# A one-core mLSTM and attention trunk: zero products ahead of TensorE's queue, the first scale row on SP's queue, far loads held back

## The chip, the cores and the metric

The kernel runs on one core of a Trainium2 chip. The metric is the device time of one execution in microseconds (us). TensorE (PE) multiplies matrices, VectorE (DVE) and ScalarE (ACT) do the elementwise work, GpSimd (POOL) and SyncE (SP) here mostly issue DMAs. PEld is TensorE's loading of the fixed operand, which overlaps its products.

## The reference

A trunk of two layers works on x (512 rows of 1024 float32). Each layer has a mixer, a cross-attention into 256 memory rows and a gated feed-forward block, and every block stands between two RMS norms:

```python
for layer in range(DEPTH):                     # DEPTH = 2
    hn = rms_norm(x, g[0])
    y = mlstm_mixer(hn, ...) if layer % 2 == 0 else stick_breaking_mixer(hn, ...)
    x = x + rms_norm(y, g[1])
    y = memory_cross_attention(rms_norm(x, g[2]), mem_n, ...)
    x = x + rms_norm(y, g[3])
    y = swiglu_ffn(rms_norm(x, g[4]), ...)
    x = x + rms_norm(y, g[5])
def rms_norm(x, gain):
    return x * rsqrt(mean(x * x) + 1e-6) * gain
```

## The kernel before

Every float32 operand of a product is split into a rounded high part and the remaining low part, and one product is made of three (low by high, high by low, high by high). ACT makes the high part with a cast, DVE the low part with a subtraction (`split`, `halves`). Most of the large products use `seven`: a 2 by 2 block product in seven block products in place of eight. It loads three of four weight blocks with SP and lets POOL add the fourth onto a block that is already there, in place, by an accumulating DMA (`gather`). So a `gather` has to wait until every reader of the block is done. In `seven` one PSUM bank `w` collects several block products, and between two of them its partial sum is copied out to a half-size buffer (`aside`).

The program is written as a list of operations in program order. `Plan.lay_out` gives them their place: it keeps a planned clock for PE, DVE, ACT, POOL and SP, and at each step takes the operation that can start first, by rank (when PE will want its result). Buffers come from a few slots per kind: 44 `big` (128 rows of 1024 floats), 8 `half`, 2 `gain` (a row of scales spread over 128 partitions, for the norms), 64 `sm`, 8 `ps` (PSUM banks). The order that comes out is fixed: each engine runs its own list strictly in that order, and a slot that is not free makes the engine wait, and with it all that stands behind on that engine.

At the start x comes in four tiles of 128 rows on SP's queue, the first in two halves, and between them come the first weights (`w_tm` of `ml_w_in`). Tile by tile `arrive` normalises (`sumsq` on ACT, a chain of small DVE and ACT operations, then on DVE x times scale times gain), turns the tile over with TensorE (`transpose_half`, the products of line 519), and splits the result; then come the first products (line 505). The gain row of this first norm, `g0`, is loaded by POOL. The mixer's gates are worked out beside this on a few rows: ACT copies a bank of 36 rows, DVE runs scans over 4 rows, and TensorE turns the result over in ten and four small products (4x4).

Of the kernel before, what the change touches and what calls it, by code (L numbers as in the profile page):

```python
# [8 lines left out]
F32 = mybir.dt.float32  # L9
R = mybir.dt.float32r  # L10
# [6 lines left out]
P = 128  # L17
D = 1024
S = 512
# [26 lines left out]

BY_DMA = (1, 3, 4)
LATER = 1000
OS = 4000
QUARTERS = (1, 6)  # L50
PROJECT = (1, 0, 1, 1, 1, 2, 0, 0)
# [79 lines left out]
class Plan:  # L131
# [63 lines left out]
    def lay_out(self):  # L195
# [25 lines left out]
                        b.lacks += sum(d not in b.group for d in o.deps)  # L221

        def feasible(o, e, headrank):
            t = max(free[e], o.ready)
            need = {}
            for b in o.bufs:
                if b.slot is None and b.kind in SLOTS:
                    need[b.kind] = need.get(b.kind, 0) + 1
                    if b.lacks and o.rank > headrank:
                        return None  # L230
            for k, n in need.items():
                s = slots[k]
                ahead, spare = SCARCE.get(k, (0, 0))
                if o.base <= headrank + ahead:
                    spare = 0
                elif spare and o.base > headrank + 25000:
                    return None
                if len(s) < n + spare:
                    return None
                t = max(t, s[n + spare - 1][0] + 60)  # L240
            return t
# [3 lines left out]
        while left:  # L245
            while head < len(pe_order) and pe_order[head].start is not None:
                head += 1
            headrank = pe_order[head].rank if head < len(pe_order) else float("inf")
            for e in free:
                found = None  # L250
                n = 0
# [26 lines left out]
            e = min((x for x in free if best[x]), key=lambda x: best[x][0], default=None)  # L278
# [6 lines left out]
            t, o = best[e]  # L285
# [87 lines left out]
class Trunk:  # L373
# [383 lines left out]
            self.ts(b[:, i : i + 1], ss, m / D, m * EPS, ALU.mult, ALU.add)  # L757
        return b[:, 0:1], b[:, 1:2]

    def gain(self, row):  # L760
        g = self.plan.buf("gain", (P, D))
        self.dma("POOL", g, row.broadcast_to([P, D]))
        return g

    def prenorm(self, out, x, g, steps=False):
        ss = self.small(1)
        self.sumsq(x, ss)
        if steps:
            v, r = self.small(1), self.small(1)
            self.ts(v, ss, 1.0 / D, EPS, ALU.mult, ALU.add)  # L770
            self.rsqrt(r, v)
        else:
            r = self.rstd(ss, D)
        self.stt(out, x, r, g, ALU.mult, ALU.mult)
# [365 lines left out]
    def stick(self, h, w_qkv, w_out, filler, finish):  # L1140
# [92 lines left out]
        def open_pair(qk):  # L1233
            z, sp = {}, {}
            for e in range(2):
                s = {}
                for b, parts in (("c", ((e, 2, 0),)), ("b", ((e, 1, 0), (e, 3, 384))), ("a", ((e, 0, 0),))):
                    z[b, e], s[b] = scores(parts, qk), self.half(S)
                    sp[b, e] = tiles(S)
                    softplus(z[b, e], s[b], sp[b, e][:, 0 : z[b, e].free])  # L1240

                u = s["c"][:, 128:256]
                self.tt(u, u, s["b"][:, 384:512], ALU.add)
                self.split(sp["c", e][:, 256:384], u)
            return z, sp

        ot, os_, qk = [], [], [project(0), project(1)]
        for p in range(KD):
            z, sp = open_pair(qk[p])
            with self.sooner(OS):  # L1250
                for o in ot[len(os_):]:
                    os_.append(self.both((S,)))
                    self.split(os_[-1], o)
            with self.later(LATER):
                for _ in range(PROJECT[p]):
# [271 lines left out]
def trunk_kernel(tc, x, mem, mem_norm_gain, norm_gains, ml_w_in, ml_b_gate, ml_head_gain, ml_w_out,  # L1527
                 sb_w_qkv, sb_w_out, xa_w_q, xa_w_kv, xa_w_o, ffn_w_gate_up, ffn_w_down, out):
    k = Trunk()
    x, mem, out = x[0], mem[0], out[0]  # L1530
    depth = norm_gains.shape[0]
    mem_gain = mem_norm_gain.rearrange("(o d) -> o d", o=1)

    def g(layer, i):
        return k.gain(norm_gains[layer, i : i + 1])

    xin = [k.big(D) for _ in range(NT)]
    for c in (slice(0, 512), slice(512, D)):
        k.dma("SP", xin[0][:, c], x[0:P, c], 700)
    for t in range(1, NT):  # L1540
        k.dma("SP", xin[t], x[t * P : (t + 1) * P])
    g0 = g(0, 0)
    k.constants()
    h = k.blocks()

    def arrive(t):
        if t:
            k.prenorm(xin[t], xin[t], g0)
            k.transpose_into(h, t, xin[t])
            return  # L1550

        ss, halves = k.small(2), [slice(0, 512), slice(512, D)]
        for i, c in enumerate(halves):
            k.sumsq(xin[t][:, c], ss[:, i : i + 1])
        r = k.rstd(ss[:, 1:2], D, k.rest(ss[:, 0:1]))
        for i, c in enumerate(halves):
            k.stt(xin[t][:, c], xin[t][:, c], r, g0[:, c], ALU.mult, ALU.mult)
            k.transpose_half(h, t, xin[t][:, c], i)

    spill = None  # L1560
    for layer in range(depth):
        j = layer // 2
        nxt, kt = {}, []

        def filler(n):

            if n and "m" not in nxt:
                nxt["m"] = k.memory(mem, mem_gain)
            for hh in range(len(kt), min(XAH, len(kt) + n)):
                kt.append(k.memory_keys(nxt["m"], xa_w_kv[layer], hh))  # L1570

        def after_mixer(n, t, ps):
            if "f" not in nxt:
                if "m" not in nxt:
                    nxt["m"] = k.memory(mem, mem_gain)
                xs = []
                for tt in range(NT):
                    xt = k.big(D)
                    k.dma("POOL", xt, x[tt * P : (tt + 1) * P] if spill is None else spill[tt])
                    xs.append(xt)  # L1580
                nxt["xs"] = xs
                nxt["h"] = k.blocks()
                nxt["f"] = k.boundary(xs, g(layer, 1), g(layer, 2), nxt["h"])
            nxt["f"](n, t, ps)

        if layer % 2 == 0:
            k.mlstm(h, arrive, ml_w_in[j], ml_b_gate[j : j + 1], ml_head_gain[j : j + 1], ml_w_out[j], filler, after_mixer)
        else:
            k.stick(h, sb_w_qkv[j], sb_w_out[j], filler, after_mixer)
        xs, h = nxt["xs"], nxt["h"]  # L1590
        nxt2 = {}

        def after_cross(n, t, ps):
            if not nxt2:
                nxt2["h"] = k.blocks()
                nxt2["x"] = [k.plan.buf("dr", (P, D)) for t in range(NT)]
                nxt2["f"] = k.boundary(xs, g(layer, 3), g(layer, 4), nxt2["h"], spill=nxt2["x"])
            nxt2["f"](n, t, ps)

        k.cross(XORDER[layer], h, nxt["m"], kt, filler, xa_w_q[layer], xa_w_kv[layer], xa_w_o[layer], after_cross)  # L1600
        h = nxt2["h"]
        nxt3 = {}

        def after_ffn(ys):
            xs = [k.big(D) for _ in range(NT)]
            for x, kept in zip(xs, nxt2["x"]):
                k.dma("POOL", x, kept)
            if layer == depth - 1:
                return k.boundary(xs, g(layer, 5), None, None, ys=ys, out=out)
            nxt3["h"] = k.acts()  # L1610
            nxt3["x"] = [k.plan.buf("dr", (P, D)) for t in range(NT)]
            return k.boundary(xs, g(layer, 5), g(layer + 1, 0), nxt3["h"], ys=ys, spill=nxt3["x"])

        k.ffn(UNITS[layer], h, ffn_w_gate_up[layer], ffn_w_down[layer], after_ffn)
        if layer < depth - 1:
            h, spill = nxt3["h"], nxt3["x"]
    k.plan.lay_out()
    k.plan.emit(tc)
# [24 lines left out]
```

## Time and profile before

| | |
|---|---|
| three runs | 1495.31, 1495.33, 1497.83 us; median 1495.33 |
| the profiled execution | 1499.86 us, of which the span of its instructions is 1498.2 |
| busy in the span | PE 1470.4 us (98%), DVE 1214.7 (81%), ACT 863.6 (58%), POOL 142.6 (10%) |
| DMA | 190.46 MB, mean 127 GB/s |
| chain that ended last | PE 31% of the span, all other engines together under 1% |

Matmuls are pipelined, so "busy" on PE is not the same as running at its peak. Idle time of an engine that nobody waits for costs nothing. Where a row names a releaser (`<-`), it is the one whose signal came last.

### The profile page before, as it was taken

The page shows a single profiled execution, that of the slowest core. Times are in us where ns is not written, and L with a number is a line of the kernel's source. Part 1 is how long each engine was busy: PE and PEld are TensorE (multiplying, and loading weights), DVE is VectorE, ACT ScalarE, POOL GpSimd, SP SyncE. Part 2 cuts the span into 40 slices and gives each one's busy share as a digit, 9 for nine tenths or more (in the row PEclk, how much of TensorE's full clock was granted, in tenths as well). Part 3 has the DMA queues.
Part 4 walks back from the last instruction along what each step waited for, and adds up shares of the span by engine and source line. Part 5 has one row for each costly group of instructions (what it writes and reads, how often), then busy time and mean ns, then how long its engine had stood idle before and what let it go on. Part 6 is the DMA issues. An engine that isn't in the chain of part 4 may idle for free. (4 is left out here: it accounts for less than half of the span.)

```text
span 1498.2 us, 26046 instructions
## 1 busy us (share of the span) xinstructions
PE 1470.4 (98%) x10346; PEld 1372.4 (92%) x10346; DVE 1214.7 (81%) x1920; ACT 863.6 (58%) x1533; POOL 142.6 (10%) x179
## 2 busy tenths in 40 slices
PE   6999899999999999999999999999999999999998
PEld 5999889998999999998889889888988999999996
DVE  7978879797887876888858998879787969768985
ACT  6668746474754454635548897756456635444632
POOL 2100100100111110110100000000000111110110
PEclk9999999999999999999999999999999999999999
DMA  7545747342654665565511215336514573854651
GB/s 240 113 85 115 223 129 237 71 128 85 203 107 100 132 150 129 118 145 187 166 32 29 71 45 182 113 119 175 143 57 140 116 167 58 205 119 86 141 170 56
DMA packets 166810, 190.46 MB, mean 127 GB/s; under 512 B 6944, under 2 KB 140576, under 8 KB 166688
## 3 DMA queue, kind: packets, MB, share of 16 engines
q1 hardware_dynamic: 119632, 121.16, 25.4%
q0 software_dynamic: 47056, 67.64, 23.0%
q8 instruction: 81, 1.33, 0.4%
q14 instruction: 41, 0.34, 0.1%
HBM read 176.72 MB, written 10.49 MB: 125 GB/s over the span
## 5 line engine op out<-in xcount | busy, mean ns | idle before, releaser
L505 PE MATMUL ps<-big,big 128*128 128x256 f32 (+2 forms) x9712 | 1407.3, 305 | 7.0 <-ACT big L436 3.5
L505 PEld LDWEIGHTS ps<-big,big 128*128 128x128 f32 x9712 | 1294.1, 189 | 93.5 <-ACT big L436 3.9
L451 DVE TENSOR_TENSOR big<-big,big 128x1024 fp32r<-128x1024 f32 (+1 forms) x516 | 607.2, 1210 | 48.9 <-ACT big L436 30.0
L436 ACT CAST big<-big 128x1024 fp32r<-128x1024 f32 (+1 forms) x385 | 391.2, 1044 | 139.9 <-DMA big<-in_ffn_w_gate_up_dram 42.1
L429 ACT ACTIVATE half<-ps 128x512 f32<-128x512 f32 (+4 forms) x185 | 92.5, 527 | 108.0 <-PE ps L505 99.7
L436 ACT COPY half<-ps 128x512 f32<-128x512 f32 (+2 forms) x105 | 61.4, 585 | 137.6 <-PE ps L505 124.9
L451 DVE TENSOR_TENSOR big<-ps,big 128x512 fp32r<-128x512 f32 (+3 forms) x188 | 109.6, 603 | 32.5 <-ACT big L436 20.3
L436 ACT CAST big<-ps 128x512 fp32r<-128x512 f32 (+2 forms) x164 | 80.2, 516 | 91.8 <-PE ps L505 55.2
L451 DVE TENSOR_TENSOR big<-half,big 128x512 fp32r<-128x512 f32 (+3 forms) x150 | 82.7, 575 | 9.3 <-ACT big L429 7.6
L429 ACT ACTIVATE half<-big 128x512 bf16<-128x512 f32 (+1 forms) x63 | 41.9, 665 | 73.1 <-DVE big L451 47.0
L418 POOL DMA_DIRECT2D big<-in_ffn_w_gate_up_dram x40 | 50.8, 1271 | 330.6 <-DVE big L451 171.1
L463 DVE SCALAR_TENSOR_TENSOR half<-ps,half 128x512 f32<-128x512 f32 (+3 forms) x74 | 47.2, 644 | 42.0 <-ACT half L436 22.3
L436 ACT CAST big<-half 128x512 fp32r<-128x512 f32 (+3 forms) x109 | 51.9, 529 | 23.1 <-DVE half L451 14.6
L519 PE MATMUL ps<-const,big 128*128 128x128 f32 (+1 forms) x314 | 44.2, 280 | 13.0 <-DVE big L463 9.9
L451 DVE TENSOR_TENSOR half<-ps,half 128x512 f32<-128x512 f32 (+2 forms) x78 | 46.9, 630 | 11.7 <-PE ps L505 8.1
L519 PEld LDWEIGHTS ps<-const,big 128*128 128x128 f32 (+1 forms) x314 | 37.9, 146 | 18.7 <-issue 10.3
L429 ACT ACTIVATE half<-half 128x512 f32<-128x512 f32 (+2 forms) x74 | 40.4, 588 | 21.1 <-DVE half L451 21.0
L451 DVE TENSOR_TENSOR big<-ps,gain 128x512 f32<-128x512 f32 x32 | 22.0, 686 | 33.4 <-ACT half L429 32.9
L429 ACT ACTIVATE big<-ps 64x512 fp32r<-64x512 f32 (+2 forms) x66 | 38.9, 590 | 11.9 <-PE ps L505 8.1
L505 PE MATMUL ps<-big,const 128*128 128x256 f32 (+3 forms) x224 | 40.5, 320 | 0.0
L505 PEld LDWEIGHTS ps<-big,const 128*128 128x128 f32 x224 | 35.6, 188 | 3.7
L463 DVE SCALAR_TENSOR_TENSOR big<-big,sm,gain 128x512 f32<-128x512 f32 (+1 forms) x47 | 36.3, 805 | 2.6 <-DMA gain<-in_norm_gains_dram 2.0
(85 smaller groups left out, 590.2 us busy)
## 6 DMA issues: line engine op xcount, KB each, us to landing
big<-in_ffn_w_gate_up_dram SPq DMA_DIRECT2D x68, 512.0 KB, 5.7
big<-in_ffn_w_gate_up_dram POOLq DMA_DIRECT2D x40, 512.0 KB, 6.0
big<-in_ffn_w_down_dram SPq DMA_DIRECT2D x36, 512.0 KB, 5.8
big<-in_xa_w_kv_dram SPq DMA_DIRECT2D x32, 512.0 KB, 5.3
big<-in_sb_w_qkv_dram SPq DMA_DIRECT2D x24, 512.0 KB, 3.9
big<-in_ml_w_in_dram SPq DMA_DIRECT2D x19, 512.0 KB, 5.5
dr<-big POOLq DMA_DIRECT2D x16, 512.0 KB, 4.9
big<-in_xa_w_o_dram SPq DMA_DIRECT2D x16, 512.0 KB, 6.2
```

What stands on the lines that cost most here:

```text
L418: "POOL", 1040, lambda nc: nc.gpsimd.dma_start(ap(out), ap(in_), accum_op=ALU.add), [in_, out], [out], load=ns
L429: nc.scalar.activation(ap(out), ap(in_), func, scale=ap(scale), **kw)
L436: "ACT", 0.833 * n + (60 if psum else 95), lambda nc: nc.scalar.copy(ap(out), ap(in_)), [in_], [out],
L451: self._dve(out, [a, b], lambda nc: getattr(nc, q).tensor_tensor(out=ap(out), in0=ap(a), in1=ap(b), op=op), eng)
L463: lambda nc: nc.vector.scalar_tensor_tensor(out=ap(out), in0=ap(a), scalar=ap(s), in1=ap(b), op0=op0, op1=op1),
L505: nc.tensor.matmul(ap(out), lhsT=ap(a), rhs=ap(b), start=start, stop=stop, **kw)
L519: nc.tensor.transpose(ap(out), ap(in_), ap(ident))
```

## The change

Three edits. (1) `warm` clears a half-size buffer on POOL and puts 18 products of that buffer with itself (128x128 by 128x512, into a bank that nobody reads) at the head of TensorE's list; `plan.pe` is set back to 0 afterwards, so that no due time moves. (2) `g0` is issued on SP behind the two halves of x's first tile, ahead of everything else on that queue, in place of POOL. (3) In `lay_out`, a load of SP or POOL whose place in PE's planned time is more than 60,000 ns ahead of where PE stands may not be issued yet.

```diff
+WARM = 18
+HOLD = 60000
...
         def feasible(o, e, headrank):
+            if o.load and e in ("SP", "POOL") and o.base > headrank + HOLD:
+                return None
...
-    def gain(self, row):
+    def gain(self, row, eng="POOL"):
         g = self.plan.buf("gain", (P, D))
-        self.dma("POOL", g, row.broadcast_to([P, D]))
+        self.dma(eng, g, row.broadcast_to([P, D]))
         return g
+
+    def warm(self, n):
+
+        z, ps = self.half(S, dt=R), self.bank()
+        self.memset(z.bitcast(F32), 0.0)
+        self.mms([(ps, z[:, 0:P], z, True, True)] * n)
+        self.plan.pe = 0.0
...
+    k.warm(WARM)
     xin = [k.big(D) for _ in range(NT)]
     for c in (slice(0, 512), slice(512, D)):
         k.dma("SP", xin[0][:, c], x[0:P, c], 700)
+    with k.sooner(3000):
+        g0 = k.gain(norm_gains[0, 0:1], "SP")
     for t in range(1, NT):
         k.dma("SP", xin[t], x[t * P : (t + 1) * P])
-    g0 = g(0, 0)
     k.constants()
```

A planner that starts from other times lays out other orders, so rows move that the diff does not name. Buffers are numbered through, and all numbers are two higher after the change. On SP's queue, at the start, before:

```order
L413 DMA big_1_68<-in_x_dram 128x512 x2
L413 DMA big_46_73<-in_ml_w_in_dram 128x2x512
L413 DMA big_2_84<-in_x_dram 128x1024
L413 DMA big_57_87<-in_ml_w_in_dram 128x2x512
L413 DMA big_3_91<-in_x_dram 128x1024
L413 DMA big_68_94<-in_ml_w_in_dram 128x2x512
```

And now:

```order
L418 DMA big_3_68<-in_x_dram 128x512 x2
L418 DMA gain_7_103<-in_norm_gains_dram 128x1024
L418 DMA big_48_106<-in_ml_w_in_dram 128x2x512
L418 DMA big_4_108<-in_x_dram 128x1024
L418 DMA big_59_111<-in_ml_w_in_dram 128x2x512
L418 DMA big_5_113<-in_x_dram 128x1024
```

The gain row stands third; every later load of this queue stands one place further back, and POOL's list has lost it.

On DVE, some 40 us into the program, where the gate work begins (`half_87` is the copy of the 36 gate rows, `big_131` a weight block of a `seven`, which a `gather` overwrites later; its readers are `big_142<-...` and the low part `big_141<-...`), before:

```order
L463 SCALAR_TENSOR_TENSOR big_26_223<-big_25_221,big_26_223 128x1024
L451 TENSOR_TENSOR big_142_494<-big_129_115,big_131_122 128x1024
L451 TENSOR_TENSOR half_87_496<-ps_86_425,half_87_496 36x512
L451 TENSOR_TENSOR big_36_166<-ps_82_413,big_35_168 128x2x256
L437 CAST big_143_530<-big_142_494 128x1024
```

And now (`half_89` and `big_133` are the same two buffers):

```order
L456 TENSOR_TENSOR big_128_492<-big_29_320,big_127_441 128x1024
L456 TENSOR_TENSOR big_144_505<-big_131_154,big_133_161 128x1024
L456 TENSOR_TENSOR half_89_512<-ps_88_444,half_89_512 36x512
L456 TENSOR_TENSOR big_38_188<-ps_84_432,big_37_197 128x2x256
L456 TENSOR_TENSOR big_143_543<-big_133_161,big_142_355 128x1024
L456 TENSOR_TENSOR big_149_545<-big_131_154,big_148_490 128x1024
```

The low part of the block (`big_141` before, `big_143` now) stood sixteen rows ahead of the gate rows' operation before; now it stands behind two readers of PSUM banks, and the block's `gather` stands behind it.

On ACT, a little later (the cast of that block after its `gather`, the two last gate operations `half_99`, `half_90`, and the copy `half_145<-ps_132` of the bank `w` by `aside`), before:

```order
L436 CAST big_148_601<-big_131_122 128x1024
L436 COPY half_145_638<-ps_132_498 128x512
L436 CAST half_99_203<-half_89_617 4x512
L429 ACTIVATE half_90_664<-half_90_664 4x512
L436 CAST big_113_683<-half_137_564 128x2x256
L436 CAST big_175_703<-big_153_479 128x1024
L436 CAST big_162_708<-big_130_131 128x1024
L436 COPY half_159_726<-ps_154_648 128x512
```

And now:

```order
L441 CAST big_150_644<-big_133_161 128x1024
L441 CAST half_101_228<-half_91_617 4x512
L434 ACTIVATE half_92_664<-half_92_664 4x512
L441 COPY half_161_672<-ps_156_624 128x512
L441 CAST big_115_693<-half_139_594 128x2x256
L441 CAST big_172_709<-big_166_638 128x1024
L441 COPY half_147_728<-ps_134_514 128x512
```

The copy of `w` (`half_145`, now `half_147`) has moved behind the gate operations and behind the next bank's copy. It follows a move on TensorE: the 24 products into `w` that it copies stood ahead of 36 other products and of the gate's small transposes, and now stand right behind those transposes and right ahead of the next 24 products into the same bank. On POOL the loads of ten other gain rows stand later in the list than before.

## Rows read from the trace of the kernel before

**Rows 1.** The page: the span and PE's busy time.

```profile
span 1498.2 us, 26046 instructions
PE 1470.4 (98%) x10346; PEld 1372.4 (92%) x10346; DVE 1214.7 (81%) x1920; ACT 863.6 (58%) x1533; POOL 142.6 (10%) x179
```

**Rows 2.** Chain that ended last, in order of time: its longest piece.

```profile
1165.36 325.48 PE ps L505 x2616
```

**Rows 3.** TensorE's timeline at the start: start, duration, instructions, idle before.

```profile
13.52 2.93 PE L505 MATMUL ps<-big,big 128*128 128x512 f32 x6
16.25 1.91 PE L519 MATMUL ps<-const,big 128*128 128x128 f32 x8
17.81 4.83 PE L505 MATMUL ps<-big,big 128*128 128x512 f32 x18
22.48 1.04 PE L519 MATMUL ps<-const,big 128*128 128x128 f32 x8
23.27 7.22 PE L505 MATMUL ps<-big,big 128*128 128x512 f32 x30
```

**Rows 4.** Timeline of the first 15 us: ACT and DVE.

```profile
4.47 0.63 ACT L429 ACTIVATE half<-big 128x512 bf16<-128x512 f32 x1
...
6.10 0.94 DVE L463 SCALAR_TENSOR_TENSOR sm<-sm,sm 128x1 f32<-128x1 f32 x1
...
9.03 0.75 DVE L463 SCALAR_TENSOR_TENSOR big<-big,sm,gain 128x512 f32<-128x512 f32 x1 [1.98 <-DMA gain<-in_norm_gains_dram]
...
9.66 1.05 ACT L436 CAST big<-big 128x1024 fp32r<-128x1024 f32 x1 [3.90 <-DMA big<-in_ml_w_in_dram]
```

**Rows 5.** Windows of 10 us: stretch, length, busy engines in turn, PEclk, DMA, GB/s.

```profile
10.00:20.00 10.00, 8.33 (x30) 6.75 (x31) 7.97 (x18) 8.78 (x20) 0.52 (x1) 1.00 1.06 376
20.00:30.00 10.00, 10.00 (x49) 8.24 (x48) 9.48 (x17) 7.49 (x13) 0.85 (x1) 1.00 0.48 161
...
40.00:50.00 10.00, 10.00 (x76) 9.36 (x74) 10.00 (x11) 7.36 (x9) 1.72 (x1) 1.00 0.36 72
50.00:60.00 10.00, 10.00 (x92) 9.85 (x90) 9.87 (x25) 6.47 (x10) 1.27 (x1) 1.00 1.05 243
```

**Rows 6.** Timeline 36 to 62 us: the gate work on ACT and TensorE, one gather.

```profile
44.23 0.58 ACT L436 COPY half<-ps 36x512 f32<-36x512 f32 x1 [2.16 <-PE ps L505]
...
45.40 0.67 DVE L451 TENSOR_TENSOR half<-ps,half 36x512 f32<-36x512 f32 x1
45.41 1.06 ACT L436 CAST big<-big 128x1024 fp32r<-128x1024 f32 x1
45.78 1.72 POOL L418 DMA_DIRECT2D big<-in_ml_w_in_dram  x1 [14.71 <-DVE big L451]
...
57.06 0.63 ACT L429 ACTIVATE half<-half 4x512 f32<-4x512 f32 x1
...
58.95 0.78 PE L519 MATMUL ps<-const,big 4*128 4x4 f32 x10
```

**Rows 7.** DMA issues of 45 to 47 us, then of 153.5 to 154.5: us to landing.

```profile
big<-in_ml_w_in_dram POOLq DMA_DIRECT2D x1, 512.0 KB, 6.5
...
big<-in_ml_w_in_dram POOLq DMA_DIRECT2D x1, 512.0 KB, 9.9
```

**Rows 8.** Groups by line: DVE's use of gain rows.

```profile
L463 DVE SCALAR_TENSOR_TENSOR big<-big,sm,gain 128x512 f32<-128x512 f32 (+1 forms) x47 | 36.3, 805 | 2.6 <-DMA gain<-in_norm_gains_dram 2.0
```

**Rows 9.** TensorE's timeline near 165 us and near 684 us.

```profile
164.94 0.38 PE L505 MATMUL ps<-big,big 128*128 128x256 f32 x1 [1.54 <-ACT big L436]
166.20 5.28 PE L505 MATMUL ps<-big,big 128*128 128x256 f32 x23 [0.88 <-DVE big L451]
...
684.83 1.42 PE L505 MATMUL ps<-big,big 128*128 128x256 f32 x10 [1.97 <-ACT big L436]
```

**Rows 10.** Windows around 168 us, columns as above.

```profile
165.00:168.00 3.00, 2.12 (x9) 1.93 (x10) 2.86 (x8) 3.00 (x8) 0.00 (x0) 0.58 1.04 414
168.00:172.00 4.00, 4.00 (x21) 4.00 (x20) 1.97 (x4) 1.12 (x2) 0.53 (x1) 0.50 1.03 406
```

## The prediction

> **What bounds the kernel now.** The page comes first: PE is busy for 1470.4 of the span's 1498.2 us [rows 1], so 27.8 us of idle is all that a schedule could win outright, and it lies at the two ends and in a few holes. Then the chain that ended last: over its last stretch TensorE issues 2616 products in 325.48 us, 124 ns each, with nothing between [rows 2]. There it waits for nobody, and an edit elsewhere can't help. So I look for places where TensorE waits or runs slowly, and the first is the head. Its timeline shows the first product at 13.52 us [rows 3]. From start to start, six products of 512 columns take 2.73 us and eight turning products 1.56; later eight turning products take 0.79. The 30 products at 23.27 have 7.22 us, so at most 241 ns each, and the first six had 455: the first is the 2.4 GHz level, the second the 1.2 GHz level (the PEclk column prints 1.00 up there, so I go by the spacing). The 18 products in between take 4.67 us, 0.33 more than 18 times 241 ns: one or two of them are still slow, so the level rises near 18.5, some 5.0 us after the first product.
>
> Why does it start so late? The timeline of the other engines tells: DVE has the tile's scale at 6.10 + 0.94 = 7.04 us and waits 1.98 us more for the gain row; ACT waits 3.90 us for the first weights, until 9.66 [rows 4]. Last the windows: DVE is busy 7.97 of the 10 us from 10 on, 9.48 in the next ten, and 10.00 and 9.87 from 40 to 60 us [rows 5]. Over the first 60 us TensorE can get ahead only as far as DVE does.
>
> **Edit by edit.** *The gain row on SP.* x's first tile is there at 4.47, where ACT starts on its second half [rows 4]. At the 376 GB/s of the 10 to 20 us window [rows 5] the 512 KB of gain behind it take 1.4 us and land near 6.0, before the scale is ready. The first scaling starts at 7.04 instead of 9.03: 2.0 us. The weights behind, another 1.4 us, land near 7.5 instead of 9.66: 2.2 us. The first product, which needs both, moves from 13.52 to about 11.4.
>
> The Trainium skill, "DMA: Bandwidth & Descriptors", section "Rules for kernel authors", says that spreading DMAs over SP, ACT and GpSimd doesn't help, since all run on the same 16 engines and interleave. By that rule, moving a load between queues gains nothing, the 2.0 us would be 0, the head below -1.0 and the whole sum +1.2 us; the rows show a gain row that came late although it was issued early, which is a matter of order rather than of bandwidth.
>
> *The zero products.* They follow a short clearing on POOL, so start near 1.6 us. For the 5.0 us seen above 11 of them take 455 ns, and seven at 241 ns follow: they end near 8.3 us, against transposes that could start at 7.8 and a first product at 11.4. They cost nothing as long as that product waits for its operands; without that cover, and at 455 ns throughout, they end at 9.8 and cost 2.0 us. What they can win is the half-rate stretch: 6 products (1.3 us), 8 turning products (0.8) and the 0.3 of the 18: 2.4 us [rows 3].
>
> *The head's sum.* At most 2.0 + 2.4 = 4.4 us. But DVE must come along: it starts 2.0 us earlier and had 2.03 us of idle in the 10 to 20 us window [rows 5], so it can be between 2.0 and 4.0 us earlier. I take the middle, **-3.0 us**.
>
> *The order that moved with it.* Near 44 us the gate work begins: ACT copies the gate rows at 44.23 (call this T), ends its last gate operation at 57.06 + 0.63 = 57.69, and the small transposes come at 58.95, with TensorE busy up to there [rows 6]. In the new order 24 products no longer stand ahead of the transposes: at 124 ns [rows 2] that is 3.0 us, so TensorE arrives at T + 11.7. One cast of 1.06 us leaves ACT's chain [rows 6], so this is ready at T + 12.4: a wait of 0.7 us that wasn't there. Second, the block's `gather` used to go out at 45.78, T + 1.6. Now it stands behind three DVE operations that begin once the gate copy is done: 0.6 + 0.67 + 0.67 us and a third over twice as many columns, about 1.2, so T + 3.1 [rows 6]. A gather lands 6.5 us after its issue in this place, and 9.9 in a crowd of other loads [rows 7]: T + 9.6 to T + 13.0. ACT's cast of the block (1.06) and the two gate operations behind it (0.63 each) end at T + 11.9 to T + 15.3, so TensorE's wait is 0.7 at best, 3.6 at worst. I take 1.4, nearer to the row of this place. Third, the copy of the bank `w` now lies between two runs of products into it with nothing to cover it: its 0.58 us (as the copy at 44.23) and signals on both sides. Bounds are 0, if the operands of the second run are later still, and 1.0; I take 0.8. Together **+2.2 us**, bounds 0.7 and 4.6.
>
> *Loads held back.* POOL's early gain loads wait in its list for a slot, and in the whole program DVE waits for gain rows 2.6 us, of which 2.0 are the first one's [rows 8]. Nobody waits behind them, and a hold of 60 us of planned time is long against a load: 0, unless a transfer lands in a crowd.
>
> *The sum.* -3.0 + 2.2 = -0.8 us. The profiled execution took 1499.86, so it would be 1499.1; the median of the runs is 1495.33, so **1494.5 us**. What a measurement of this kernel can tell from no change is about 0.2%, 3.0 us: this is no change.
>
> **What widens it.** In the profiled execution TensorE idled 1.54 and 0.88 us near 165 us [rows 9], and its clock then ran at half for the whole of 168 to 172 and most of the window before [rows 10], about 6.5 us, worth up to 3.3 us. Near 684 us it idled 1.97 us and the rate didn't fall [rows 9]. Whether it falls hangs on where the hole lies, and the change moves every hole by a few us, in both directions. The three runs of before differ by 2.5 us.
>
> **Rivals.** *A: the clock falls back.* Between the zeros' end (8.3) and the first product (11.4) TensorE has only eight transposes to do: over 2 us of idle, between the hole that cost the rate and the one that didn't [rows 9]. If it falls and takes 6.5 us to return [rows 10], against 5.0 us at half rate after the first product now, the zeros lose 0.8 us instead of winning; the head is -2.0 + 0.8 = -1.2, the sum +1.0: 1496.3. A gain row that lands no earlier than before ends in the same place, and is counted here. The Trainium skill, "TensorE: Matmul & The Clock Gate", section "Part 4: PE-mode transpose", says that the full rate doesn't engage for transposes, so they would not hold the clock up; the trace disagrees at least for the rate, since eight turning products take 1.04 us at 22.48 [rows 3], and no run here shows whether they keep it.
>
> *B: the give-back is smaller.* If the gather lands early and TensorE is held by DVE at that place anyway, only 0.7 of the 2.2 us remains, and if DVE uses all of its early idle, the head is -4.0: -3.3, so 1492.0. For it speaks that TensorE had no idle between 20 and 60 us [rows 5]; against it that DVE had next to none either.
>
> *C: slower.* The gather meets other loads and lands after 9.9 us, as it did at 153.9 [rows 7]. TensorE then idles 3.6 us near 56 us in one piece, more than the hole that cost the rate at 165 us, and the 6.5 us at half rate cost 3.3 us more: -3.0 + 3.6 + 0.8 + 3.3 = +4.7, 1500.0. It decides from a hole of about 2.4 us on, so from a landing later than about 8.7 us after issue.
>
> **Chances.** The forecast 0.45 (its own range 1492.5 to 1496.5), A 0.18, B 0.25, C 0.12. B lies beyond 0.2% faster, C beyond 0.2% slower, the other two within: faster 0.25, same 0.63, slower 0.12. The range leaves out half of C, and a far B: 1491.0 to 1498.5.
>
> **What the profile after would show.** Eighteen products of zeros from about 1.6 us; the first scaling near 7.0 without a wait for the gain row; the first real product near 11.4, and from there on 241 ns a product if the clock held, 455 if A is right; the third tile's transposes near 19.5 instead of 22.48. Then, near 53 to 56 us, a hole of 0.7 to 3.6 us on TensorE ahead of the small transposes, with ACT's cast behind a gather as its cause, and a shorter one ahead of the second run into the bank `w`; a lead of about 3 us before and about 1 after. No wait for a gain row on DVE. Wrong would be: no hole there (B), a hole that takes the clock with it (C), or a load that lands late because of the hold, which I cost at nothing.

## The result, and the profile after

The changed kernel is slower: 1503.8 us in the median of six runs (1502.74 to 1507.8) against 1495.61 in six of the kernel before, ratio 1.0051, 95% interval 1.004 to 1.0062. Some 8 us are lost where the forecast was no change, 1494.5 us, with 1498.5 as its upper end.

The profiled execution of the changed kernel took 1502.74 us. Its page answers to [rows 1]: as many products as before and 18 more, 6.2 us more of PE time, the same share.

```profile
span 1501.0 us, 26081 instructions
PE 1476.6 (98%) x10364; PEld 1377.1 (92%) x10364; DVE 1215.7 (81%) x1919; ACT 863.0 (57%) x1534; POOL 143.4 (10%) x179
```

Start with TensorE's timeline of the head, against [rows 3]: start, duration, instructions, idle before and its releaser.

```profile
1.57 6.43 PE L510 MATMUL ps<-half 128*128 128x512 f32 x18 [1.57 <-POOL half L487]
8.63 1.38 PE L524 MATMUL ps<-const,big 128*128 128x128 f32 x8 [0.63 <-DVE big L468]
12.58 2.73 PE L510 MATMUL ps<-big,big 128*128 128x512 f32 x6 [2.58 <-ACT sm L434]
15.11 1.56 PE L524 MATMUL ps<-const,big 128*128 128x128 f32 x8
...
20.71 1.03 PE L524 MATMUL ps<-const,big 128*128 128x128 f32 x8
```

The zeros end at 8.00. Then TensorE turns one tile over and idles 2.58 us, and the six first products take from start to start 2.53 us: they run at the lower level all the same. The first product comes 0.9 us earlier than at 13.52, the third tile's transposes 1.8 us earlier than at 22.48. DVE's timeline, against [rows 4]:

```profile
7.73 1.57 DVE L468 SCALAR_TENSOR_TENSOR big<-big,sm,gain 128x512 f32<-128x512 f32 x2 [1.24 <-DMA gain<-in_norm_gains_dram]
```

And ACT's, with its gate copy:

```profile
9.06 1.05 ACT L441 CAST big<-big 128x1024 fp32r<-128x1024 f32 x1 [1.94 <-DMA big<-in_ml_w_in_dram]
...
42.45 0.58 ACT L441 COPY half<-ps 36x512 f32<-36x512 f32 x1 [2.58 <-PE ps L510]
```

The gain row is there at 7.7 in place of 9.0 and is still waited for, 1.24 us; the first weights come 0.6 us earlier. The gate copy starts at 42.45, against 44.23 in [rows 6]: a lead of 1.8 us. Now TensorE where the gate work ends, and a row near 170 us.

```profile
54.45 0.78 PE L524 MATMUL ps<-const,big 4*128 4x4 f32 x10
57.99 0.58 PE L524 MATMUL ps<-const,half 4*128 4x4 f32 x4 [2.76 <-ACT half L434]
58.50 5.49 PE L510 MATMUL ps<-big,big 128*128 128x256 f32 x24
64.72 3.45 PE L510 MATMUL ps<-big,big 128*128 128x256 f32 x27 [0.73 <-ACT half L441]
...
170.46 0.38 PE L510 MATMUL ps<-big,big 128*128 128x256 f32 x1 [2.09 <-ACT big L441]
```

A hole of 2.76 us, then 24 products in 5.49 us, 229 ns each where [rows 2] has 124, then 0.73 us of idle for the copy of the bank `w`. The last row is the first of [rows 9], there at 164.94: the lead of 1.8 us has become a lag of 5.5, 7.3 us in all. The hole, the half rate (24 products at 229 in place of some 129 ns: 2.4 us) and the copy are 5.9 of these, the longer hole in the last row 0.55; the other 0.85 is not accounted for. ACT's timeline tells why:

```profile
55.84 1.04 ACT L441 CAST big<-big 128x1024 fp32r<-128x1024 f32 x1 [6.05 <-DMA big<-in_ml_w_in_dram]
56.79 0.61 ACT L441 CAST half<-half 4x512 fp32r<-4x512 f32 x1
57.31 0.62 ACT L434 ACTIVATE half<-half 4x512 f32<-4x512 f32 x1
...
64.08 0.58 ACT L441 COPY half<-ps 128x512 f32<-128x512 f32 x1 [4.22 <-PE ps L510]
```

So do the DMA issues from 45.5 to 49 us (KB each, us to landing):

```profile
big<-in_ml_w_in_dram SPq DMA_DIRECT2D x3, 512.0 KB, 8.5
big<-in_ml_w_in_dram POOLq DMA_DIRECT2D x1, 512.0 KB, 9.7
```

ACT waits 6.05 us in its first row for the `gather` on POOL's queue, issued at 46.13 and landed 9.7 us later, with three SP loads beside it. The two gate operations (the rows at 56.79 and 57.31) stand behind that cast in ACT's list, and TensorE stands behind them. Their operand is ready at 54.2, as DVE's timeline shows:

```profile
53.54 0.68 DVE L456 TENSOR_TENSOR half<-big,half 4x512 f32<-4x512 f32 x1
```

The windows show the clock (columns as in [rows 5]):

```profile
13.00:16.00 3.00, 3.00 (x11) 2.41 (x10) 2.96 (x4) 3.00 (x5) 0.00 (x0) 0.50 1.04 404
57.20:64.00 6.80, 6.00 (x28) 5.69 (x28) 5.43 (x6) 2.67 (x5) 0.00 (x0) 0.50 0.16 26
...
168.00:172.00 4.00, 1.03 (x7) 0.63 (x6) 1.49 (x4) 2.63 (x6) 0.00 (x0) 1.00 1.04 412
```

TensorE runs at 1.2 GHz from 13 to 16 us and from 57.2 to 64. Near 170 us it idles but keeps 2.4 GHz, where the profiled execution of before fell [rows 10]: the two profiled executions differ by 2.9 us only, the medians by 8.2.

### The profile page after: what moved, and what is told of

It is laid out like the page before. It is cut to its first block, busy times and chain, and to the rows that moved or that the text cites. A ratio compares the mean times of both kernels' runs of the same rounds, so it can differ in the third digit from the quotient of the medians.

```text
span 1501.0 us, 26081 instructions
## 1 busy us (share of the span) xinstructions
PE 1476.6 (98%) x10364; PEld 1377.1 (92%) x10364; DVE 1215.7 (81%) x1919; ACT 863.0 (57%) x1534; POOL 143.4 (10%) x179
## 5 line engine op out<-in xcount | busy, mean ns | idle before, releaser
L441 ACT CAST big<-half 128x512 fp32r<-128x512 f32 (+4 forms) x111 | 52.2, 523 | 23.5 <-DVE half L456 14.9
```

What stands on the lines that cost most here:

```text
L441: "ACT", 0.833 * n + (60 if psum else 95), lambda nc: nc.scalar.copy(ap(out), ap(in_)), [in_], [out],
```

## The experiments

**Each edit alone.** The theory: the loss comes from the order that was laid out anew, and that comes from the gain edit. Rivals: it comes from the zeros, or from the hold. TensorE's list of warm_only differs from before in the zeros alone, that of hold_only in nothing, and that of gain_only in the move of the 24 products told ahead of the prediction. The diff below takes the three edits back, out of the changed kernel: the hold, the gain row (its lines are in two places) and the zeros. warm_only takes back the hold and the gain row, hold_only the gain row and the zeros, no_gain the gain row, gain_only the hold and the zeros.

```diff
-HOLD = 60000
+HOLD = 1e12
...
-    with k.sooner(3000):
-        g0 = k.gain(norm_gains[0, 0:1], "SP")
...
+    g0 = g(0, 0)
...
-    k.warm(WARM)
```

*warm_only.* 

> Only the zero products; gain row back on POOL, no hold. The order of the 44 to 66 us stretch is that of the kernel before. Theory T (the loss comes from the order that was laid out anew at 44 to 66 us): the gate copy near 44.2 us as before, no hole ahead of the gate's small transposes, time 1494 to 1497.5. Theory Z (the loss comes from the zeros and the clock that falls back after them): six slow products at the first tile as before, the clock at half again later, and some 1501 to 1504 us.

*gain_only.* 

> Only the gain row third on SP's queue; no zeros, no hold. This alone lays out the order of the changed kernel at 44 to 66 us. Theory T: a hole of 2 to 4 us on TensorE ahead of the gate's small transposes, the clock at half behind it, the exposed copy of the bank w, and 1501 to 1505 us. Theory Z, or a theory of the hold: 1493 to 1497 us, the hole without a price in the end.

*hold_only.* 

> Only the hold of far loads; no zeros, gain row on POOL. No product changes its place on TensorE's list. Theory T: no change, 1494.5 to 1497. Theory H (a held load lands late, later in the program): slower by 3 us or more, with waits for a DMA that the kernel before does not have.

*no_gain.* 

> The changed kernel with the gain row back on POOL: zeros and hold alone, the order at 44 to 66 us as before. Theory T: 1494 to 1497.5, so putting this one load back gives back the whole loss of 8 us. Theories Z and H: most of the loss stays, 1500 to 1504.

| kernel | median us | ratio to before, 95% |
|---|---|---|
| gain_only | 1503.52 | 1.0044 (1.0031 to 1.0056) |
| warm_only | 1498.46 | 1.002 (1.0011 to 1.0029) |
| hold_only | 1496.82 | 1.0005 (0.9996 to 1.0013) |
| no_gain | 1498.6 | 1.0015 (1.0004 to 1.0027) |

The hold is free. The gain edit carries 6.6 us (0.0044 of 1496). But the zeros cost 2 to 3 us of their own, which the theory did not have: warm_only and no_gain lie above its range and below the rivals'. TensorE's timeline of gain_only at the gate:

```profile
58.72 0.59 PE L524 MATMUL ps<-const,half 4*128 4x4 f32 x4 [2.85 <-ACT half L434]
59.24 5.44 PE L510 MATMUL ps<-big,big 128*128 128x256 f32 x24
65.41 4.87 PE L510 MATMUL ps<-big,big 128*128 128x256 f32 x39 [0.73 <-ACT half L441]
```

A window of gain_only behind it:

```profile
60.00:64.00 4.00, 4.00 (x21) 4.00 (x20) 4.00 (x4) 0.60 (x1) 0.00 (x0) 0.50 0.00 0
```

The same hole, half rate and copy, without any zeros.

**The order mended.** Each operation has its number in program order; `move` takes one out of the finished order and puts it behind another. cast_later is the changed kernel with one row of ACT moved, gain_two_moves is gain_only with that row moved and two casts put behind the copy of `w`.

```diff
+    def move(self, what, behind):
+        at = {o.seq: o for o in self.order}
+        self.order.remove(at[what])
+        self.order.insert(self.order.index(at[behind]) + 1, at[what])
...
     k.plan.lay_out()
+    k.plan.move(252, 204)
```

```diff
     k.plan.lay_out()
+    k.plan.move(250, 202)
+    k.plan.move(234, 244)
+    k.plan.move(290, 234)
```

*cast_later.* 

> The changed kernel with one row moved: ACT's cast of the gathered block stands behind the two last gate operations instead of ahead of them. Theory T (TensorE idles near 55 us because the gate operations stand behind a cast that waits for the gather): the idle time ahead of the last four small transposes falls from 2.76 to below 1.2 us, TensorE's clock is not at half in the 10 us behind it, and most of the 6.6 us that the gain row alone costs comes back: 1496.5 to 1500. Rival S (the same wait is met one step later, at the next products that need the gathered block): the hole moves there, the clock falls all the same, 1501.5 to 1504.

*gain_two_moves.* 

> The gain row third on SP's queue, no zeros and no hold, laid out anew as in gain_only, but two rows of ACT moved: the cast of the gathered block behind the two last gate operations, and the copy of the bank w ahead of two casts that stood in front of it. Theory T (those waits are all that the new order costs): no hole above 1.2 us between 50 and 62 us, the clock not at half there, the copy's hole near 0.7 us instead of 1.62, and 1494.5 to 1497. Rival S (other rows of the new order cost time too): 1498.5 or more.

cast_later took 1500.27 us, ratio 1.0032 (1.0019 to 1.0045); its profiled execution 1496.82. gain_two_moves took 1497.34, 1.0006 (0.9998 to 1.0015). Both medians are 0.3 us above theory T's range; cast_later still holds the 18 zeros and the longer hole at the copy. TensorE's timeline of cast_later:

```profile
54.02 0.78 PE L529 MATMUL ps<-const,big 4*128 4x4 f32 x10
54.66 0.38 PE L529 MATMUL ps<-const,half 4*128 4x4 f32 x4
54.98 3.09 PE L515 MATMUL ps<-big,big 128*128 128x256 f32 x24
59.69 10.55 PE L515 MATMUL ps<-big,big 128*128 128x256 f32 x87 [1.62 <-ACT half L446]
```

Two windows of cast_later:

```profile
57.00:60.00 3.00, 1.38 (x12) 1.18 (x11) 2.76 (x3) 3.00 (x6) 0.00 (x0) 1.00 0.24 38
60.00:64.00 4.00, 4.00 (x36) 4.00 (x35) 4.00 (x5) 3.67 (x5) 0.00 (x0) 1.00 0.02 4
```

TensorE's timeline of gain_two_moves, its last two rows there:

```profile
56.20 3.12 PE L515 MATMUL ps<-big,big 128*128 128x256 f32 x24
60.05 10.16 PE L515 MATMUL ps<-big,big 128*128 128x256 f32 x84 [0.73 <-ACT half L446]
```

The hole ahead of the four transposes is gone, the 24 products take 3.1 us, and the clock holds; what remains is the copy's hole, 1.62 us, and 0.73 with the two casts out of its way. In both kernels the `gather` lands as late as before the mending (10.4 and 10.1 us after its issue): here late data cost little once nothing urgent is queued behind them. In gain_two_moves the loss of gain_only goes from 0.44% to 0.06%, and the intervals don't meet. Rival S is out.

**The order of before kept.** gain_kept is the kernel before with one row moved: after the layout, operation 5 (the gain row) stands behind operation 1 and goes out on SP. both_kept has 18 zero products at the head as well (the line of `zeros`), both_kept_more 11 more behind the first tile's transposes; zeros_32 and zeros_6 are both_kept with other numbers.

```diff
     k.plan.lay_out()
+    k.plan.move(5, 1)
+    k.zeros(18)
+    first = k.plan.order[[o.seq for o in k.plan.order].index(5)]
+    first.fn = lambda nc: nc.sync.dma_start(ap(g0), norm_gains[0, 0:1].broadcast_to([P, D]))
```

```diff
-    k.zeros(18)
+    k.zeros(18, 38, 11)
```

*gain_kept.* 

> The kernel before with every row in its place but one: the gain row is issued third on SP's queue instead of by POOL. Theory T (the load itself is harmless, the order laid out after it costs the time): the first scaling near 7.5 us, the third tile's transposes 1 to 2 us earlier than at 22.48, the gate copy that much ahead of 44.23, no hole ahead of the gate's small transposes, and 1493.5 to 1496.5. Rival G (the load on SP's queue costs the time by what it holds back behind it): 1499 or more.

*both_kept.* 

> As gain_kept, and 18 zero products at the head of TensorE's list, all other rows in their places. Theory T: 1493 to 1496. Theory Z2 (zeros cost some 2.5 us wherever they stand, as in the run with zeros alone, since TensorE's lead is given back at a later hole and the clock falls there): 1496.5 to 1499, a clock at half at 165 or 684 us or later.

*both_kept_more.* 

> As both_kept, with 11 more zero products behind the first tile's transposes, to bridge TensorE's idle time until the first real product. If the clock's fall back in the head is what spoils the zeros (rival A of the prediction): the first six products take 1.5 us instead of 2.7, eight turning products 0.8 instead of 1.6, and the whole 1 us or more less than both_kept. If DVE sets the head's pace: the third tile's transposes no earlier than in both_kept, and the same time within 1 us.

*zeros_32.* 

> As both_kept, with 32 zero products instead of 18, which end near 11 us and leave TensorE little idle time before the first real product. Theory A (the clock's fall back near 13 us spoils them): six products in 1.5 us, the third tile's transposes no later than in both_kept, and a median about 1 us below that of both_kept, 1498.9. Theory Z3 (zeros cost by their number): 1500 or more.

*zeros_6.* 

> As both_kept, with 6 zero products instead of 18, too few to raise the clock for the first real products. Theory Z3 (zeros cost by their number): near 1497, a third of both_kept's loss. Theory Z4 (any product that early costs it): 1498.5 to 1499.5. If the loss hangs on the clock that rises early: as gain_kept, 1496.2.

*zeros_32_again.* 

> zeros_32 once more, on the same chip as both_kept. If it matters that the clock doesn't fall back in the head: 1 to 2 us below both_kept. If 18 and 32 zeros cost alike: the same within 0.7 us.

*both_kept_third.* 

> both_kept once more, beside the three kernels below, so that they can be compared. If the loss with 18 zeros is a property of the kernel: 1498 to 1499.5, ratio 1.001 to 1.0025. If it came from the chip or the hour: 1496 to 1497, as the kernel before.

| kernel | median us | ratio to before, 95% |
|---|---|---|
| gain_kept | 1496.18 | 1.0004 (0.9995 to 1.0013) |
| zeros_6 | 1496.21 | 1.001 (1.0 to 1.0019) |
| both_kept | 1498.87 | 1.0018 (1.0009 to 1.0027) |
| both_kept_third | 1498.43 | 1.0016 (1.0006 to 1.0025) |
| zeros_32 | 1497.12 | 1.0007 (0.9998 to 1.0016) |
| zeros_32_again | 1496.47 | 1.0 (0.9991 to 1.0009) |
| both_kept_more | 1500.26 | 1.0034 (1.0021 to 1.0048) |

gain_kept: the load itself harms nothing, but the expectation of an earlier head missed, as DVE's timeline shows:

```profile
8.63 0.75 DVE L468 SCALAR_TENSOR_TENSOR big<-big,sm,gain 128x512 f32<-128x512 f32 x1 [2.41 <-DMA gain<-in_norm_gains_dram]
11.00 1.23 DVE L456 TENSOR_TENSOR big<-big,big 128x1024 fp32r<-128x1024 f32 x1 [1.62 <-ACT big L441]
12.14 0.75 DVE L468 SCALAR_TENSOR_TENSOR big<-big,sm,gain 128x512 f32<-128x512 f32 x1
```

Here the row landed 0.4 us earlier than at 9.03, and in the old order the second scaling stands behind a subtraction that waits for the weights; the third tile's transposes come at 23.15, later than at 22.48. One execution says little of this: in two of both_kept the first scaling starts at 8.58 and at 7.37. In the new order both scalings follow each other (x2 at 7.73), so part of what the head won came with that order, as the loss did.

18 zeros cost 2.5 us here too, twice, and 32 zeros cost nothing that the two measurements show: the cost does not grow with the number. Six leave it open: the median is that of gain_kept, but three of eleven executions took 1499.9 or more. The added work of both_kept_more stood in the way: the first tile's second transposes came at 12.98, not near 10, so its 11 products ran from 13.43 and delayed the first real product to 17.59. It tells nothing of the clock. zeros_32 does: its six first products take 1.66 us (2.86 in both_kept), so the clock held, and then TensorE waits for DVE ahead of the third tile's transposes, which come 0.5 us earlier than both_kept's 22.15:

```profile
21.62 1.09 PE L524 MATMUL ps<-const,big 128*128 128x128 f32 x8 [0.92 <-DVE big L468]
```

**Where executions with 18 zeros lose.** both_kept's profiled execution (1497.32) was shorter than its median; a second execution of the same program shows where the longer ones lose.

*both_kept_again.* 

> A second look at both_kept, whose profiled execution (1497.32) was shorter than its median (1498.87): where does an execution with zeros lose 2 us or more? If the clock falls at TensorE's holes near 165, 684 and 1430 us are the cause: a stretch at half rate behind one or more of them. If not: a wait or a start that the other profile does not have.

It took 1500.56 us. A window of the first execution:

```profile
684.00:688.00 4.00, 4.00 (x30) 3.73 (x29) 4.00 (x7) 3.44 (x6) 0.00 (x0) 1.00 1.04 390
```

The `gather` that it waits for, among the first execution's DMA issues near 667 us:

```profile
big<-in_ffn_w_down_dram POOLq DMA_DIRECT2D x1, 512.0 KB, 7.2
```

The same window of the second execution:

```profile
684.00:688.00 4.00, 3.76 (x20) 3.79 (x21) 4.00 (x5) 3.04 (x4) 0.00 (x0) 0.62 0.38 98
```

The same load in the second execution:

```profile
big<-in_ffn_w_down_dram POOLq DMA_DIRECT2D x1, 512.0 KB, 11.7
```

And TensorE's timeline in the second execution:

```profile
684.24 5.99 PE L510 MATMUL ps<-big,big 128*128 128x256 f32 x30 [3.24 <-ACT big L441]
```

The same program, the same load: landed after 7.2 us it leaves no hole, after 11.7 it leaves one of 3.24 us and a clock of 0.62 behind it. Near 165 us both executions have a hole (2.39 and 2.35 us) and a fall. All five profiled executions with just 18 zeros in the order of before fall there (three of both_kept, warm_only, no_gain), but those of gain_kept and before, without zeros, do too. Near 684 us only two of these five fall (no_gain's has 0.67), and no profiled execution without zeros does. That a hole brings a fall is no law: hold_only, whose TensorE list is that of before, idled longer there than the 1.54 us of [rows 9] (0.88 us more follow in both) and kept the full rate. TensorE's timeline of hold_only:

```profile
165.18 0.38 PE L510 MATMUL ps<-big,big 128*128 128x256 f32 x1 [1.93 <-ACT big L441]
```

A window of hold_only behind it:

```profile
168.00:172.00 4.00, 4.00 (x37) 4.00 (x36) 4.00 (x7) 3.39 (x7) 0.53 (x1) 1.00 1.03 404
```

**The holes filled.** both_fill is both_kept with 14 small products of a cleared 256-column buffer, into a PSUM bank that is free there, ahead of the late products near 165 us and near 684 us; before_fill is the kernel before with these fills alone.

```diff
+    k.z = k.const(P, 256, dt=BF16)
+    k.memset(k.z, 0.0)
+    k.plan.order[0:0] = k.plan.ops[-1:]
+    k.fill(14, 717, 6)
+    k.fill(14, 2396, 6)
```

*both_fill.* 

> As both_kept, and 14 small products of zeros where TensorE idles near 165 us and 14 where it idles near 684 us, each ahead of the products whose operands are late. Theory F (the zeros' loss is half-rate stretches behind those two holes): no half rate at 165 and 684, and 1 to 2.5 us below both_kept, so 1496 to 1497.5. If the loss is elsewhere: as both_kept, 1498.5 or more.

*before_fill.* 

> The kernel before with the same two fills and nothing else. Theory F: it too falls to half rate near 165 us in some executions, so 0.5 to 1.5 us below before, 1494.5 to 1495.5. If the fills come in the way of late operands or the falls are too rare: 1495.5 to 1497, no difference.

both_fill took 1495.0 us, 0.9996 (0.9987 to 1.0005), against 1.0016 (1.0006 to 1.0025) for both_kept_third on the same chip; before_fill 1496.63, 1.0004 (0.9992 to 1.0015). TensorE's timeline of both_fill:

```profile
162.47 1.70 PE L510 MATMUL ps<-const 128*128 128x256 bf16 x14
164.67 0.38 PE L510 MATMUL ps<-big,big 128*128 128x256 f32 x1 [0.49 <-ACT big L441]
...
679.59 1.70 PE L510 MATMUL ps<-const 128*128 128x256 bf16 x14
```

A window of both_fill:

```profile
165.00:168.00 3.00, 2.13 (x18) 2.08 (x18) 2.86 (x9) 3.00 (x7) 0.00 (x0) 1.00 1.04 413
```

With the fills the zeros' loss is gone, and in this execution the rate holds: theory F stands for the zeros, though the two intervals only just part (1.0005 and 1.0006), and which of the two fills does it was not tried. It fails for the kernel before, which gains nothing: in before_fill's profiled execution the clock fell near 168 us behind the fill and 0.67 and 0.87 us of idle.

**Everything at once.** mended is gain_two_moves with 18 zeros, 11 more behind the first tile's transposes, and both fills; zeros_32_fill is both_fill with 32 zeros.

```diff
     k.plan.move(290, 234)
+    k.zeros(18, 38, 11)
...
+    k.fill(14, 717, 6)
+    k.fill(14, 2396, 6)
```

*mended.* 

> gain_two_moves (the gain row on SP, the new order with its two rows of ACT mended) with 18 zero products at the head, 11 more behind the first tile's transposes, and the two fills near 165 and 684 us. If all losses are named: a lead of 1.5 to 2 us at 40 us as in the changed kernel, at most 1.5 of it given back at 55 to 60 us, no half rate between 13 and 1480 us, and 1493.5 to 1495.5, 8 us or more below the changed kernel. If something is missing: 1497 or more.

*zeros_32_fill.* 

> both_fill with 32 zero products instead of 18, so that the clock does not fall back in the head. If the fall in the head still costs both_fill something: 1494 to 1494.7. If the head is set by DVE and the loads: 1494.7 to 1496, as both_fill.

mended took 1496.08 us, 1.0004 (0.9996 to 1.0013), 0.6 above its range; zeros_32_fill 1495.18, 0.9994 (0.9985 to 1.0003), as both_fill. TensorE's timeline of mended in the head:

```profile
9.56 1.23 PE L529 MATMUL ps<-const,big 128*128 128x128 f32 x8 [0.77 <-DVE big L473]
10.54 2.77 PE L515 MATMUL ps<-big 128*128 128x512 f32 x11
13.64 1.62 PE L515 MATMUL ps<-big,big 128*128 128x512 f32 x6 [0.33 <-DVE big L461]
...
20.53 1.03 PE L529 MATMUL ps<-const,big 128*128 128x128 f32 x8
```

A window of mended over it:

```profile
10.00:20.00 10.00, 9.62 (x47) 7.27 (x46) 9.21 (x19) 9.30 (x20) 0.00 (x0) 1.00 1.07 374
```

Here the clock holds through the head (the six first products take 1.62 us), and yet the third tile's transposes come at 20.53, only 0.2 us before those of the changed kernel, where it fell. With zeros_32's wait for DVE this says that DVE and the loads set the head's pace. Within that interval, 0.9996 to 1.0013, the named causes are all of the loss, and nothing of the hoped gain can be measured: no version beats the kernel before beyond its interval.

## Why the prediction was wrong, step by step

**The step that failed** is the price of the re-laid order, "I take 1.4, nearer to the row of this place": that wait measured 2.76. The `gather` landed after 9.7 us, near the other row of [rows 7], 9.9, and the half rate behind the hole, for which the forecast's sum had no term, cost 2.4 us more. That was the rival with the smallest chance, C: hole 3.6 us (it was shorter, as TensorE still did the ten transposes until T + 12.8, where the forecast had it waiting from T + 11.7), copy 0.8 (0.73), half rate 3.3 (2.4), all in the place named. The row of 6.5 us was one without neighbours. The next three SP loads, in the kernel before:

```profile
50.31 5.57 SPq L413 DMA_DIRECT2D big<-in_ml_w_in_dram  x3
```

And in the changed one, 0.4 us ahead of the `gather` in place of 4.5 behind it:

```profile
45.73 3.23 SPq L418 DMA_DIRECT2D big<-in_ml_w_in_dram  x3
```

They were read as "one place further back" on the queue, not as earlier in time. In every profile with the order of before this `gather` lands after 6.5 to 7.0 us, in the five with the new order after 9.5 to 10.4. That the SP loads beside it are the cause is argued from this; no run held them back alone. That ACT's order made the late `gather` expensive is shown, by moving one row.

**The head's -3.0** was -1.8 at the gate copy. The gain row was reckoned to land near 6.0 and landed at 7.7; the weights near 7.5, and came at 9.0. The reckoning took the 376 GB/s of the 10 to 20 us window for both; between 4 and 7 us the changed kernel's DMA moved 182, 221 and 309 GB/s in the three microseconds. "A matter of order" was at most part of it: third on its queue, issued at 1.72 us, the gain row still took 5.9 us to land, against 7.6 before. Either edit alone brings the gate copy to 43.1 (gain_only 43.10, warm_only 43.14), but two executions of both_kept differ by 1.1 us there.

**The zeros** ran from 1.57 to 8.00 us as forecast (1.6 to 8.3). The forecast counted the rise from the first product at 13.52, but eight transposes, at 9.93 and 12.68, stand ahead of it in the kernel before. Then rival A came true: 2.58 us of idle, and the first products at the lower level. Its price was small, as mended and zeros_32 show; but "they cost nothing as long as that product waits" missed some 2.5 us that the fills near 165 and 684 us took back, far from the head.

**The rule on queues** was the prediction's counter-case to the 2.0 us: the Trainium skill, "DMA: Bandwidth & Descriptors", section "Rules for kernel authors", has it that spreading DMAs over SP, ACT and GpSimd for bandwidth doesn't help. For the load alone the runs agree: gain_kept is 1.0004 (0.9995 to 1.0013), and its row landed 0.4 us earlier.

**The hold at nothing** was right, 1.0005 (0.9996 to 1.0013). Of [rows 8], though, 2.6 us is DVE's idle time ahead of all these operations, and 2.0 of it, the first row's, is what it waits for gain rows.

**The copy of `w`** at 0.8 was right (0.73).

**The size.** C's sum was 1500.0. In the profiled executions the re-laid order gave back 7.3 us by 170 us, near C's 7.7, and the head's lead was 1.8 in place of 3.0: a lag of 5.5, where the medians differ by 8.2. The rest is not settled. The zeros' 2.5, a difference of medians, would bring the sum to 8.0, but the changed kernel's profiled execution, the fastest of its six, shows nothing of it: from the last row near 170 us to the end of its span it takes 1330.5 us, and hold_only from the same products on 1329.8. The ratios of the single edits add up to 0.69% (0.44, 0.20 and 0.05), against 0.51% (0.40 to 0.62) for all three. The profiled execution of before was a poor measure: it took 4.25 us more than the median of its runs, with a fall at 165 us that hold_only's lacks.

## What to carry to other kernels

Where a planner lays out the order, an edit of one load is an edit of the whole list: read what stands behind each DMA wait on each in-order engine, and move urgent small work ahead of it; here three moved rows were worth 0.38% (gain_only against gain_two_moves), some 5.7 us, more than the 4.4 us that the prediction gave the head at most. Price a wait for a load by the traffic that will run beside it in the new schedule, not by its row in the old one. A microsecond won in the head need not show in the end: here none of the kernels that had it was measurably faster.

## What the runs showed of the hardware

The same accumulating load of 512 KB landed after 7.2 us in one execution and after 11.7 in another of the same program, and after 6.5 to 10.4 at the gate, by kernel. TensorE kept 2.4 GHz behind a hole of 1.93 us near 165 us in hold_only and fell to 1.2 behind 1.54 at the same place in the profiled execution of before, so the hole's length alone does not decide (0.88 us of idle follow in both). And 18 products of zeros made a kernel 0.16 to 0.2% slower in three measurements, though they end 3 us and more before the first real product, while 32 of them did not measurably (1.0 and 1.0007); two fills near 165 and 684 us took that back. Why 18 of them bring more loss at those holes stays open.
